# Gate and up of a decoder's feed-forward: weights as the stationary operand, both parts of the activations as the moving one

## The chip, the core and the metric

The kernel runs on one core of a Trainium2 chip. Its engines are TensorE (PE; matrix products, with its weight loads listed apart as PEld), VectorE (DVE), ScalarE (ACT), GpSimd (POOL) and SyncE (SP, which here issues the transfers from memory). Each works through its own list of instructions in order, and they wait for one another by semaphores. The metric is the time of one execution in microseconds (us) on the device; lower is better. All inputs are float32.

## The reference, cut to what matters

Two layers, each a mixer (attention) and a feed-forward, over a residual stream x of 256 tokens by 1024 columns. The mixers are left out here. The feed-forward's inner width D_FF is 2816.

```python
def rmsnorm(x, g):
    xf = x.astype(jnp.float32)
    y = xf * lax.rsqrt(jnp.mean(xf * xf, axis=-1, keepdims=True) + NORM_EPS)
    return (y * g.astype(jnp.float32)).astype(x.dtype)

def swiglu(h, w_gate, w_up, w_down):
    return (jax.nn.silu(h @ w_gate) * (h @ w_up)) @ w_down

def reference(...):
    for layer in range(DEPTH):          # DEPTH = 2
        h = rmsnorm(x, norm_mix[layer])
        ...                             # the mixer of this layer
        x = x + mix
        x = x + swiglu(rmsnorm(x, norm_ffn[layer]), ffn_w_gate[layer], ffn_w_up[layer], ffn_w_down[layer])
    return rmsnorm(x, norm_final)
```

## The kernel before

**Three products for one.** To keep float32's precision, each operand is split in a high part (a copy to the type fp32r, made by ACT) and a low part (the value less the high part, made by DVE). A product is then three products on PE: high by high, high activation by low weight, low activation by high weight (`mm3`, L264).

**A product on PE** has a stationary operand of 128 x 128, which a weight load brings in, and a moving operand of up to 512 columns that streams through it. The result stands in PSUM, eight banks of 128 partitions x 512 float32. The kernel shares them out: four banks `mm` (gate and the outputs), two banks `s` (up), two banks `tp` (transposes).

**Weights** come as one stream of tiles of 128 x 1024 (class `Weights`, L74): a transfer fills w_raw (5 buffers), ACT copies it to w_hi (L108), DVE subtracts into w_lo (L109; 7 buffers each). `W.next()` hands out the next tile and has up to six more prepared. The list of tiles follows FF_CHUNKS; a chunk of width w has 1024 / w slices of the model width in one tile.

**The norm** (`Norm.half`, L226) takes one half of 512 columns of one block of 128 tokens as soon as the residual of that half is done: DVE multiplies by the gain (xg, L229), PE transposes it in four blocks (pt_a, L215), ACT and DVE split it into aT, where the model width is on the partitions (L209, L210). The scale of each token, rs, comes later from the sum of squares (ACT, DVE, POOL); products use the unscaled activations and multiply rs in afterwards. aT has a tile for each block of tokens t and each part: four tiles.

**The feed-forward** (`ffn`, L322) goes chunk by chunk through the inner units: five chunks of 512 and one of 256. For gate and then for up, the stationary operand is a block of aT (128 tokens), the moving one 512 columns of weights, so the result has tokens on the partitions and inner units along the row. Then for each t ACT takes Silu of gate with the scale rs of the token (sg, L343), DVE multiplies up by rs and by sg (hn, L344), and since the down product needs inner units on the partitions, PE transposes hn in blocks of 128 (`split_T`, L215), and ACT and DVE split that into hT_hi and hT_lo. The transposes of a chunk run on PE among the first products of the next chunk.

**The down product** (`residual`, L281) has a block of hT stationary and 512 columns of the down weights moving; its last three tiles are done half by half, so that each half's residual (x, L302) and the next norm start early.

**Order.** The order in which each engine runs its list is set by a scheduler of the framework, which places instructions by its own estimate of times; transfers stay in program order.

## Time and profile before

| | |
|---|---|
| time, median of 3 runs | 676.5 us (675.41 to 676.85) |
| the profiled execution, its own time | 676.92 us |
| its span, first to last instruction | 675.1 us |
| granted PE clock, mean | 0.993 of full speed |
| first gate product to first down product, layer 0 | 143.52 to 270.35 us |
| the same, layer 1 | 480.86 to 607.42 us |

The profile is of one execution. Times are counted from the span's start. Busy time is the time an engine worked on something; on PE the ends of products are modelled and overlap, so the distance from start to start says more than the duration. A row of a timeline has the start, the duration, engine, line, operation, output <- inputs and the shape, and in brackets how long the engine had been idle and what ended that. In grouped rows stand busy us, mean ns of one, then the idle time ahead.

### The profile page before, as it was taken

The numbers are of one execution on the slowest core, as the hardware profiler recorded it, in microseconds if no ns is written. First come the engines' busy times: TensorE is split into PE (matmuls) and PEld (weight loads), VectorE is DVE, ScalarE is ACT, GpSimd is POOL, SyncE is SP. The second block draws the span as 40 slices with busy tenths as digits, with TensorE's granted clock in tenths as the row PEclk, the third lists the DMA queues.
The fourth block names the chain that finished last, engine by engine and source line by source line (L and its number), as shares of the span: only waits on it lengthen the run. The fifth ranks groups of instructions, "written<-read, shape, count | busy, mean of one in ns | idle before, by whom it ended". The sixth has DMA issues, their size and how long they took to land.

```text
span 675.1 us, 9324 instructions
## 1 busy us (share of the span) xinstructions
PE 651.3 (96%) x3329; PEld 533.7 (79%) x3329; DVE 435.6 (65%) x954; ACT 369.5 (55%) x671; POOL 12.4 (2%) x24
## 2 busy tenths in 40 slices
PE   5999999999999999999999999969999999999996
PEld 4979788778888889888887877746788888898884
DVE  4989977767455555543588899696674555465424
ACT  4775847547444444433376687686574544444322
POOL 1000000100000000000000000000000000000000
PEclk9999999999999999999999999989999999999999
DMA  8845355138666666662386431400396555555501
GB/s 313 254 149 168 117 165 157 31 109 319 201 184 184 192 182 184 185 193 74 101 346 216 155 126 39 150 0 2 121 329 196 178 178 196 181 182 187 186 1 62
DMA packets 31869, 109.62 MB, mean 162 GB/s; under 512 B 3536, under 2 KB 3792, under 8 KB 31568
## 3 DMA queue, kind: packets, MB, share of 16 engines
q1 hardware_dynamic: 31392, 108.45, 49.5%
q8 instruction: 26, 0.43, 0.3%
q10 hardware_dynamic: 432, 0.59, 0.2%
q14 instruction: 19, 0.16, 0.1%
HBM read 107.98 MB, written 1.05 MB: 161 GB/s over the span
## 4 chain that ended last, share of the span: by engine, by line
PE 82%; ACT 6%; DMA 5%; DVE 4%; issue 2%; POOL 0%; SPq 0%; POOLq 0%; DVEq 0%; ACTq 0%
PE ps_out L265 7%; PE ps_out L267 7%; PE ps_out L266 7%; PE ps_g L267 5%; PE ps_g L266 5%; PE ps_g L265 5%; PE ps_u L266 5%; PE ps_u L267 5%; PE ps_u L265 5%; DMA w_raw<-in_w 5%; PE ps_in L265 4%; PE ps_in L267 4%; PE ps_in L266 4%; PE pt_a L215 3%; PE ps_o L822 2%
## 5 line engine op out<-in xcount | busy, mean ns | idle before, releaser
L109 DVE TENSOR_TENSOR w_lo<-w_raw,w_hi 128x1024 fp32r<-128x1024 f32 (+5 forms) x200 | 234.5, 1180 | 176.6 <-ACT w_hi L108 176.2
L108 ACT ACTIVATE w_hi<-w_raw 128x1024 fp32r<-128x1024 f32 (+5 forms) x200 | 202.9, 1024 | 203.4 <-PE ps_out L267 58.6
L265 PE MATMUL ps_in<-w_hi,aT 128*128 128x512 f32 (+5 forms) x208 | 77.5, 373 | 1.2 <-ACT aT L209 1.2
L267 PE MATMUL ps_in<-w_hi,aT 128*128 128x512 f32 (+5 forms) x208 | 77.2, 373 | 0.0
L266 PE MATMUL ps_in<-w_lo,aT 128*128 128x512 f32 (+5 forms) x208 | 76.7, 370 | 0.0
L265 PE MATMUL ps_g<-w_hi,aT 128*128 128x512 f32 (+1 forms) x192 | 72.4, 377 | 0.0
L267 PE MATMUL ps_g<-w_hi,aT 128*128 128x512 f32 (+1 forms) x192 | 71.8, 376 | 0.0
L266 PE MATMUL ps_g<-w_lo,aT 128*128 128x512 f32 (+1 forms) x192 | 71.7, 373 | 0.0
L265 PE MATMUL ps_u<-w_hi,aT 128*128 128x512 f32 (+1 forms) x192 | 71.3, 371 | 0.0
L266 PE MATMUL ps_u<-w_lo,aT 128*128 128x512 f32 (+1 forms) x192 | 71.3, 371 | 0.0
L267 PE MATMUL ps_u<-w_hi,aT 128*128 128x512 f32 (+1 forms) x192 | 71.3, 371 | 0.0
L265 PE MATMUL ps_out<-w_hi,hT_hi 128*128 128x512 f32 x176 | 69.5, 395 | 0.0
L267 PE MATMUL ps_out<-w_hi,hT_lo 128*128 128x512 f32 x176 | 69.3, 394 | 0.0
L266 PE MATMUL ps_out<-w_lo,hT_hi 128*128 128x512 f32 x176 | 68.5, 389 | 0.0
L265 PEld LDWEIGHTS ps_in<-w_hi,aT 128*128 128x128 f32 x208 | 39.9, 192 | 6.1 <-ACT aT L209 1.8
L320 ACT ACTIVATE e<-e,bias 128x128 f32<-128x128 f32 (+1 forms) x96 | 42.5, 446 | 3.1 <-DVE bias L319 3.0
L267 PEld LDWEIGHTS ps_in<-w_hi,aT 128*128 128x128 f32 x208 | 39.7, 191 | 4.5 <-DVE aT L210 0.3
L266 PEld LDWEIGHTS ps_in<-w_lo,aT 128*128 128x128 f32 x208 | 39.7, 191 | 4.4 <-issue 0.4
L265 PEld LDWEIGHTS ps_u<-w_hi,aT 128*128 128x128 f32 x192 | 36.2, 188 | 6.3
L266 PEld LDWEIGHTS ps_u<-w_lo,aT 128*128 128x128 f32 x192 | 36.2, 188 | 6.3
L267 PEld LDWEIGHTS ps_u<-w_hi,aT 128*128 128x128 f32 x192 | 36.2, 188 | 6.2
L265 PEld LDWEIGHTS ps_g<-w_hi,aT 128*128 128x128 f32 x192 | 36.2, 188 | 6.0
(208 smaller groups left out, 946.2 us busy)
## 6 DMA issues: line engine op xcount, KB each, us to landing
w_raw<-in_w SPq DMA_DIRECT2D x176, 512.0 KB, 3.6
w_raw<-in_w SPq DMA_DIRECT2D x8, 384.0 KB, 4.6
gain<-in_vec SPq DMA_DIRECT2D x4, 512.0 KB, 5.1
cw<-in_cw SPq DMA_DIRECT2D x2, 1024.0 KB, 8.2
w_raw<-in_w SPq DMA_DIRECT2D x4, 416.0 KB, 6.6
w_raw<-in_w SPq DMA_DIRECT2D x4, 328.0 KB, 6.9
w_raw<-in_w SPq DMA_DIRECT2D x4, 304.0 KB, 2.8
x<-in_x SPq DMA_DIRECT2D x4, 256.0 KB, 6.2
```

The costliest lines, as they stand in the source:

```text
L108: nc.scalar.activation(hi[:, :n], raw[:, :n], AF.Copy)
L109: nc.vector.tensor_sub(lo[:, :n], raw[:, :n], hi[:, :n])
L215: TE.transpose(pt[:, i], src[:, i * P : (i + 1) * P], ident)
L265: TE.matmul(ps, act[0][:, k], wh, start=start, stop=False)
L266: TE.matmul(ps, act[0][:, k], wl, start=False, stop=False)
L267: TE.matmul(ps, act[1][:, k], wh, start=False, stop=stop)
L320: A.activation(e, e, AF.Exp, scale=-1.0, bias=bias, accum_out=den)
L822: pin(TE.matmul(ob[64 * par : 64 * par + 64], vv[:, st, c : c + 64], pTs[par][:, b, st].rearrange("p j c -> p (j c)"), start=False, stop=l ...
```

## The change

Gate and up change roles: a block of 128 x 128 weights is stationary and the activations move, so inner units come out on the partitions, as the down product wants them, and the transposes of hn go. The activations of both parts and all 256 tokens lie in one tile aW (`new_wide`): for the high weights one product moves 512 columns (256 tokens of the high part, 256 of the low part), for the low weights one moves the 256 of the high part. High by high and low weight by high activation meet in the left half of the bank, high weight by low activation in the right half, so the two halves must be added: an ACT copy of the right half and a DVE addition, for gate and for up. The token's scale now lies along the row; it is spread over the partitions once per layer (`spread`: two products of a block of ones with a diagonal of rs), multiplied into gate by DVE, and for up it is put off to the end of the down product (`residual` with rs). All chunks are 256 wide.

```diff
@@ -27,7 +27,7 @@
 
 EV_CHUNKS = [328, 416, 384, 384, 512, 512, 512]
 OD_CHUNKS = [304, 256, 512, 512, 512, 512]
-FF_CHUNKS = [512, 512, 512, 512, 512, 256]
+FF_CHUNKS = [256] * 11
 WCOLS = 1024
 
 
@@ -205,6 +205,11 @@
     def new_aT(pool):
         return [[pool.tile([P, KD, P], F32R, tag="aT", bufs=2 * NT, name="aT") for _ in range(2)] for _ in range(NT)]
 
+    def new_wide():
+
+        w = ap.tile([P, KD, 2, T], F32R, tag="aW", name="aW")
+        return w, [[w[:, :, z, t * P : (t + 1) * P] for z in range(2)] for t in range(NT)]
+
     def split(hi, lo, src):
         A.activation(hi, src, AF.Copy)
         V.tensor_sub(lo, src, hi)
@@ -220,7 +225,7 @@
 
         def __init__(self, goff):
             self.goff = goff
-            self.aT = new_aT(ap)
+            self.wide, self.aT = new_wide()
             self.rs = [small_tile(1, "rs") for _ in range(NT)]
 
         def half(self, t, h):
@@ -278,7 +283,7 @@
                     mm3(ps[t][:, :w], aT[t], g * kk + i, wh[:, i], wl[:, i], g == 0 and i == 0, g == n - 1 and i == kk - 1)
         return ps
 
-    def residual(act, nk, tail, nxt):
+    def residual(act, nk, tail, nxt, rs=None):
 
         ps = [[mm_bank("ps_out") for _ in range(2)] for _ in range(NT)]
 
@@ -299,7 +304,10 @@
                     one(t, h, nk - tail + k, last[k])
                 if t == NT - 1 and h == 1:
                     W.prepare(W.used + 2)
-                V.tensor_add(xs[t][:, c], ps[t][h], xs[t][:, c])
+                if rs is None:
+                    V.tensor_add(xs[t][:, c], ps[t][h], xs[t][:, c])
+                else:
+                    V.scalar_tensor_tensor(xs[t][:, c], ps[t][h], rs[t], xs[t][:, c], op0=ALU.mult, op1=ALU.add)
                 nxt.half(t, h)
 
     def rope(pool, dst, src, rs, t, nb, d):
@@ -320,31 +328,58 @@
         A.activation(e, e, AF.Exp, scale=-1.0, bias=bias, accum_out=den)
 
     def ffn(nm, goff):
-        aT, rs = nm.aT, nm.rs
+        wide, rs = nm.wide, nm.rs
         gain(goff)
         nxt = Final() if goff == V_FIN else Norm(goff)
         with tc.tile_pool(name="ffn", bufs=1, reuse_waits="tile") as fp:
-            hT = [(fp.tile([P, KF, P], F32R, tag=f"hh{t}", name="hT_hi"), fp.tile([P, KF, P], F32R, tag=f"hl{t}", name="hT_lo")) for t in range(NT)]
-            k0 = 0
-            for c, w in enumerate(FF_CHUNKS):
+            hh = fp.tile([P, KF, T], F32R, tag="hh", name="hT_hi")
+            hl = fp.tile([P, KF, T], F32R, tag="hl", name="hT_lo")
+
+
+            ones = fp.tile([P, P], F32, tag="ones", name="ones")
+            V.memset(ones, 1.0)
+            rB = fp.tile([P, T], F32, tag="rB", name="rB")
+
+            def spread():
+                dg = nat("dg")
+                pb = t_bank("ps_r")
+                for t in range(NT):
+                    c = slice(t * P, (t + 1) * P)
+                    V.tensor_scalar(dg[:, c], ident, rs[t], None, op0=ALU.mult)
+                    TE.matmul(pb[:, c], ones, dg[:, c], start=True, stop=True)
+                evac(rB, pb[:, :T])
+
+            f0 = 0
+            for w in FF_CHUNKS:
                 kk = ff_kk(w)
-                n = KD // kk
-                gp = [mm_bank("ps_g") for _ in range(NT)]
-                up = [s_bank("ps_u") for _ in range(NT)]
+                nf = w // P
+                gp = [mm_bank("ps_g") for _ in range(nf)]
+                up = [s_bank("ps_u") for _ in range(nf)]
                 for dst in (gp, up):
-                    for g in range(n):
+                    for g in range(KD // kk):
                         wh, wl = W.next()
                         for i in range(kk):
-                            for t in range(NT):
-                                mm3(dst[t][:, :w], aT[t], g * kk + i, wh[:, i], wl[:, i], g == 0 and i == 0, g == n - 1 and i == kk - 1)
-                for t in range(NT):
-                    sg = fp.tile([P, 512], F32, tag="sg", bufs=2, name="sg")[:, :w]
-                    hn = fp.tile([P, 512], F32, tag="hn", bufs=2, name="hn")[:, :w]
-                    A.activation(sg, gp[t][:, :w], AF.Silu, scale=rs[t])
-                    V.scalar_tensor_tensor(hn, up[t][:, :w], rs[t], sg, op0=ALU.mult, op1=ALU.mult)
-                    split_T(hT[t], k0, hn, w // P)
-                k0 += w // P
-            residual(hT, KF, 3, nxt)
+                            k = g * kk + i
+                            for f in range(nf):
+                                c = slice(f * P, (f + 1) * P)
+                                TE.matmul(dst[f], wh[:, i, c], wide[:, k].rearrange("p z q -> p (z q)"), start=k == 0, stop=False)
+                                TE.matmul(dst[f][:, :T], wl[:, i, c], wide[:, k, 0], start=False, stop=k == KD - 1)
+                    if dst is gp and f0 == 0:
+                        spread()
+                for f in range(nf):
+                    sg = fp.tile([P, T], F32, tag="sg", bufs=3, name="sg")
+                    hn = fp.tile([P, T], F32, tag="hn", bufs=3, name="hn")
+                    evac(sg, gp[f][:, T:])
+                    V.tensor_add(sg, gp[f][:, :T], sg)
+                    V.tensor_mul(sg, sg, rB)
+                    A.activation(sg, sg, AF.Silu)
+                    evac(hn, up[f][:, T:])
+                    V.tensor_add(hn, up[f][:, :T], hn)
+                    V.tensor_mul(hn, hn, sg)
+                    split(hh[:, f0 + f], hl[:, f0 + f], hn)
+                f0 += nf
+            hT = [[z[:, :, t * P : (t + 1) * P] for z in (hh, hl)] for t in range(NT)]
+            residual(hT, KF, 3, nxt, rs)
         return nxt
 
 
```

What this does to the order of PE at the entry of the first feed-forward, first before, then after: ps_out are the last products of the mixer's output, pt_a <- xg the transposes of the second 128 tokens, ps_g the first gate products. Waits stand in brackets with the engine waited for.

```order
L265 MATMUL ps_out<-w_hi,aT 128x512
L266 MATMUL ps_out<-w_lo,aT 128x512
L267 MATMUL ps_out<-w_hi,aT 128x512
L265 MATMUL ps_g<-w_hi,aT 128x512 [waits Activation_49]
L215 MATMUL pt_a<-con,xg 128x128 [waits DVE_49,PE_49]
L215 MATMUL pt_a<-con,xg 128x128 x3
L266 MATMUL ps_g<-w_lo,aT 128x512
L267 MATMUL ps_g<-w_hi,aT 128x512
L265 MATMUL ps_g<-w_hi,aT 128x512
L266 MATMUL ps_g<-w_lo,aT 128x512
L215 MATMUL pt_a<-con,xg 128x128 [waits DVE_49,PE_49]
```

```order
L270 MATMUL ps_out<-w_hi,aT 128x512
L271 MATMUL ps_out<-w_lo,aT 128x512
L272 MATMUL ps_out<-w_hi,aT 128x512
L220 MATMUL pt_a<-con,xg 128x128 [waits DVE_49,PE_49]
L220 MATMUL pt_a<-con,xg 128x128 x3
L220 MATMUL pt_a<-con,xg 128x128 [waits DVE_49,PE_49]
L220 MATMUL pt_a<-con,xg 128x128 x3
L365 MATMUL ps_g<-aW,w_hi 128x512 [waits DVE_49]
L366 MATMUL ps_g<-aW,w_lo 128x256
L365 MATMUL ps_g<-aW,w_hi 128x512
L366 MATMUL ps_g<-aW,w_lo 128x256
```

Before, gate products on the first 128 tokens stand among the transposes of the second 128; after, both groups of transposes and a wait for DVE stand ahead of the first gate product.

DVE's list in the first feed-forward, in the middle of it, is next; first before, where one chunk of 512 has two pieces hn and two pieces hT_lo:

```order
L344 SCALAR_TENSOR_TENSOR hn<-ps_u,rs,sg 128x512 [waits PE_49] x2
L109 TENSOR_TENSOR w_lo<-w_raw,w_hi 128x1024 [waits DMAHW6_49,Activation_49]
L210 TENSOR_TENSOR hT_lo<-pt_a,hT_hi 128x512 [waits Activation_49] x2
L109 TENSOR_TENSOR w_lo<-w_raw,w_hi 128x1024 [waits DMAHW7_49,Activation_49]
L109 TENSOR_TENSOR w_lo<-w_raw,w_hi 128x1024 [waits DMAHW0_49,Activation_49]
L109 TENSOR_TENSOR w_lo<-w_raw,w_hi 128x1024 [waits DMAHW1_49,Activation_49]
L109 TENSOR_TENSOR w_lo<-w_raw,w_hi 128x1024 [waits DMAHW2_49,DVE_49,Activation_49]
L109 TENSOR_TENSOR w_lo<-w_raw,w_hi 128x1024 [waits DMAHW3_49,DVE_49,Activation_49]
L109 TENSOR_TENSOR w_lo<-w_raw,w_hi 128x1024 [waits DMAHW4_49,DVE_49,Activation_49]
L109 TENSOR_TENSOR w_lo<-w_raw,w_hi 128x1024 [waits DMAHW5_49,Activation_49]
```

And after, most of one chunk of 256 (it goes on with one more weight split and one more hT_lo): sg is gate, hn is up, ps_g and ps_u their banks, rB the spread scale.

```order
L373 TENSOR_TENSOR sg<-ps_g,sg 128x256 [waits Activation_49]
L374 TENSOR_TENSOR sg<-sg,rB 128x256 [waits DVE_49]
L109 TENSOR_TENSOR w_lo<-w_raw,w_hi 128x1024 [waits DMAHW0_49,PE_49,Activation_49]
L373 TENSOR_TENSOR sg<-ps_g,sg 128x256 [waits Activation_49]
L374 TENSOR_TENSOR sg<-sg,rB 128x256 [waits DVE_49]
L109 TENSOR_TENSOR w_lo<-w_raw,w_hi 128x1024 [waits DMAHW1_49,PE_49,Activation_49]
L377 TENSOR_TENSOR hn<-ps_u,hn 128x256 [waits Activation_49]
L378 TENSOR_TENSOR hn<-hn,sg 128x256 [waits DVE_49]
L109 TENSOR_TENSOR w_lo<-w_raw,w_hi 128x1024 [waits DMAHW2_49,PE_49,Activation_49]
L215 TENSOR_TENSOR hT_lo<-hn,hT_hi 128x256 [waits Activation_49]
L377 TENSOR_TENSOR hn<-ps_u,hn 128x256
L378 TENSOR_TENSOR hn<-hn,sg 128x256 [waits DVE_49]
```

Between one weight split (w_lo) and the next there now stand one to three pieces of 256 columns, most with a wait for ACT (Activation), where weight splits followed one another.

## Rows read from the trace of the kernel before

**Rows 1.** Page part 1: busy us (share of the span) xinstructions.

```profile
PE 651.3 (96%) x3329; PEld 533.7 (79%) x3329; DVE 435.6 (65%) x954; ACT 369.5 (55%) x671; POOL 12.4 (2%) x24
```

**Rows 2.** Windows: length, busy of PE, PEld, DVE, ACT, POOL, clock, DMA, GB/s.

```profile
143.52:270.35 126.83, 126.65 (x626) 106.00 (x624) 71.72 (x73) 64.65 (x75) 1.12 (x2) 1.00 0.66 207
480.86:607.42 126.56, 126.56 (x626) 106.01 (x624) 71.75 (x73) 64.60 (x75) 1.09 (x2) 1.00 0.62 208
507.51:530.31 22.80, 22.80 (x106) 18.75 (x105) 12.32 (x12) 10.90 (x12) 0.00 (x0) 1.00 0.56 184
```

**Rows 3.** Timeline of PE, first gate chunk of layer 1.

```profile
484.71 0.39 PE L265 MATMUL ps_g<-w_hi,aT 128*128 128x512 f32 x1
...
499.67 0.39 PE L265 MATMUL ps_u<-w_hi,aT 128*128 128x512 f32 x1
```

**Rows 4.** Timeline of PE, the chunk of 256 of layer 1.

```profile
597.10 0.28 PE L266 MATMUL ps_g<-w_lo,aT 128*128 128x256 f32 x1
...
607.18 0.28 PE L266 MATMUL ps_u<-w_lo,aT 128*128 128x256 f32 x1
```

**Rows 5.** Timeline of PE around the transposes of one chunk.

```profile
526.77 0.39 PE L266 MATMUL ps_g<-w_lo,aT 128*128 128x512 f32 x1
527.06 0.66 PE L215 MATMUL pt_a<-con,hn 128*128 128x128 f32 x4
...
528.46 0.39 PE L266 MATMUL ps_g<-w_lo,aT 128*128 128x512 f32 x1
```

**Rows 6.** Timeline of PE in the second mixer, fp32 products of 128 columns.

```profile
469.44 1.06 PE L814 MATMUL ps_o<-cT,vbd 128*128 128x128 f32 x8
470.43 1.08 PE L822 MATMUL ps_o<-pT,vv 128*64 128x512 f32 x4
```

**Rows 7.** Timeline at the entry of the second feed-forward.

```profile
480.86 0.40 PE L265 MATMUL ps_g<-w_hi,aT 128*128 128x512 f32 x1
...
481.78 0.69 DVE L229 TENSOR_TENSOR xg<-x,gain 128x512 f32<-128x512 f32 x1
...
482.44 0.69 DVE L210 TENSOR_TENSOR aT<-pt_a,aT 128x512 fp32r<-128x512 f32 x1
...
482.62 0.63 PE L215 MATMUL pt_a<-con,xg 128*128 128x128 f32 x4
...
484.02 0.40 PE L265 MATMUL ps_g<-w_hi,aT 128*128 128x512 f32 x1
...
484.88 0.55 POOL L199 TENSOR_TENSOR rs<-rs,half 128x1 f32<-128x1 f32 x1 [3.48 <-DVE rs L198]
```

**Rows 8.** Grouped rows of DVE and ACT, by form.

```profile
L109 DVE TENSOR_TENSOR w_lo<-w_raw,w_hi 128x1024 fp32r<-128x1024 f32 x176 | 213.9, 1222 | 166.0 <-ACT w_hi L108 165.5
...
L210 DVE TENSOR_TENSOR hT_lo<-pt_a,hT_hi 128x256 fp32r<-128x256 f32 x4 | 1.5, 415 | 0.0
...
L108 ACT ACTIVATE w_hi<-w_raw 128x1024 fp32r<-128x1024 f32 x176 | 185.1, 1058 | 186.0 <-PE ps_out L267 50.8 <-PE ps_u L267 50.5 <-PE ps_g L267 41.4
...
L343 ACT ACTIVATE sg<-ps_g,rs 128x256 f32<-128x256 f32 x4 | 1.9, 470 | 3.0 <-PE ps_g L267 3.0
...
L209 ACT ACTIVATE hT_hi<-pt_a 128x256 fp32r<-128x256 f32 x4 | 1.3, 371 | 0.0
```

**Rows 9.** Waits, 484 to 596 us: total us, times, longest us.

```profile
ACT w_hi L108 <- PE ps_u L267: 22.9, 14, 1.7
...
ACT w_hi L108 <- DMA w_raw<-in_w: 3.6, 2, 2.7
```

**Rows 10.** Grouped rows of DVE: residual and the old hn.

```profile
L344 DVE SCALAR_TENSOR_TENSOR hn<-ps_u,rs,sg 128x512 f32<-128x512 f32 x20 | 14.0, 744 | 0.0
...
L302 DVE TENSOR_TENSOR x<-ps_out,x 128x512 f32<-128x512 f32 x16 | 11.0, 689 | 14.2 <-PE ps_out L267 14.1
```

**Rows 11.** Grouped row of PE's weight loads.

```profile
L265 PEld LDWEIGHTS ps_u<-w_hi,aT 128*128 128x128 f32 x192 | 36.2, 188 | 6.3
```

## The prediction

> **What bounds the kernel now.** I read the engine totals of the page first. TensorE (PE) is busy 651.3 us (96% of the span) and VectorE (DVE) 435.6 (65%) [rows 1]. That busy PE is a share only; whether PE is the limit in the part that changes is read from stretches. The two stretches from the first gate product to the first down product last 126.83 and 126.56 us, and PE is busy in 126.65 and 126.56 of them, at granted clock 1.00 (the 2.4 GHz level) [rows 2]. So gate and up wait for nothing: their time is what PE is given to do. One chunk of 512 inner units takes 22.80 us there, of which DVE works 12.32 (54%) and ScalarE (ACT) 10.90 (48%) [rows 2]. The reader should keep two things: a PE instruction saved in this stage is time saved, and DVE and ACT have slack that the change is going to use.
>
> The sum is made against the profiled execution, 676.92 us (span 675.1, 1.8 outside it); the median of the three runs is 676.5, 0.4 less.
>
> **Matmuls: the same columns, cut differently.** I read the spacing of starts, since the recorded durations overlap. From 484.71 to 499.67 us lie 66 products of 512 columns: 14.96 / 66 = 0.2267 us each [rows 3]. From 597.10 to 607.18 lie 84 of 256 columns: 10.08 / 84 = 0.1200 us each [rows 4]. Columns at 2.4 GHz would be 0.2133 and 0.1067, so each product carries about 0.0133 us of its own, whatever its width.
> Before, a layer has five chunks of 96 products at 512 and one chunk of 96 at 256: 480 x 0.2267 + 96 x 0.1200 = 120.3 us. After, each of 22 unit blocks of 128 takes, for gate and for up and for each of 8 slices of the model width, one product of 512 columns (high weights; high and low activations side by side) and one of 256 (low weights; high activations): 352 pairs x (0.2267 + 0.1200) = 122.0 us. That is **+1.7 us a layer**: columns are equal (270,336), and 704 products carry their fixed part where 576 did. Bounds: without a fixed part for the added products 0.0; with the load of every pair laid bare far more (last rival). I take the two spacings added, since both stand in this stage.
>
> The Trainium skill, page "TensorE: Matmul & The Clock Gate", section "Back-to-back issue gap", gives N/2.4 + 2.5 ns between products. For 512 and 256 columns that is an estimate of 215.8 and 109.2 ns, where this trace has 226.7 and 120.0 [rows 3, 4]. By that page of the Trainium skill the step would be +0.3 us a layer instead of +1.7, and the whole sum 2.8 us better. The trace disagrees with it at both widths and decides, so +1.7 stays.
>
> **Transposes: gone.** Before, each chunk's hidden values come out with tokens on the partitions and PE turns them, 8 blocks per chunk of 512. Around one such pair of groups, three products that need 0.68 us take from 526.77 to 528.46, 1.69 us [rows 5]: 1.0 us for eight transposes; the chunk period says the same, 22.80 - 96 x 0.2267 = 1.04 [rows 2, 3]. Per layer five chunks at 1.03 and half of that for the last one, which falls into the down products: **-5.6 us a layer**. This is PE time in a stage where PE never waits, so it is path, all of it.
>
> **The broadcast of the row scale.** The change needs the scale of each token along the free axis and makes it with two fp32 products (ones times a diagonal) of 128 columns a layer. In the trace four such fp32 products (eight records) stand from 469.44 to 470.43, 0.25 us each [rows 6]: **+0.5 us a layer**. Its operand is ready long before: the second scale is done at 484.88 + 0.55 = 485.4 us [rows 7], and the first gate phase, 16 x 0.347 = 5.5 us, ends later (below). A bound above is one DVE-to-PE wait of about 1 us.
>
> **The entry into the feed-forward.** This is where something gets worse by order. Before, the first gate product needs only the first 128 tokens, and PE fills the wait for the second 128 with it: from 480.86 to 484.02 us PE issues nine products (2.04 us) and two groups of transposes, so 1.12 us go beside products [rows 7]. After, a moving operand holds both parts and all 256 tokens, so all transposes stand ahead of the first gate product. From the rows: the second group of transposes follows xg of 481.78 to 482.47 and starts at 482.62; DVE then takes the low part of the third of the four halves (of the second 128 tokens the first 512 columns) at 482.44 to 483.13 [rows 7]. A small memset (ones) now stands in DVE before that xg, say 0.15 to 0.2 us. So the first gate product starts near 483.45, 2.59 us after 480.86 and not 1.12 with products between: **+1.5 us a layer**. The next need, the fourth half of the activations, comes 2.8 us later (16 products) and is split about 484.8, ahead of need 486.2. Bounds: 1.3 (no memset) to 2.5 (one more DVE item of 0.69 ahead of the split).
>
> **The longer epilogue.** Per chunk of 256 units DVE gets four weight splits (1.222 each) and ten pieces of 128 x 256 at 0.415: 4.9 + 4.2 = 9.0 us, and ACT four weight copies (1.058), six copies of 256 columns (0.371) and two Silu (0.470): 4.2 + 2.2 + 0.9 = 7.4 us [rows 8]. A chunk lasts 32 x 0.3467 = 11.1 us on PE, so both fit, DVE at 82% where it had 54%. What PE waits for is the two banks of up, which the next chunk's up wants 5.55 us after this one ends. Following DVE's new order from that end: ACT copy of the first block 0.5, add and multiply 0.8, a weight split 1.2 (its copy on ACT runs beside), low part 0.4, second add 0.4, with handoffs 3.7 us. Margin 1.8 us, so steady chunks cost nothing. The weights keep their lead: a weight copy waits for PE to give buffers back (22.9 us in 14 waits), hardly for DMA (3.6 us, 2 waits) [rows 9]. Those two waits are at the stage's start, where ACT's copies of the gate banks now stand behind a weight copy; there the margin shrinks to about nothing in the first two chunks, and I allow 0.2 us a layer (bounds 0 and 1.5). Adding the scale in the down stage's last step costs DVE 0.744 instead of 0.689 [rows 10]; only the very last one is on the path, +0.06 in total.
>
> **Sum.** Per layer -5.6 + 1.7 + 0.5 + 1.5 + 0.2 = -1.7 us, twice -3.4, plus 0.06: -3.4. From 676.92 that is 673.5; less the 0.4 by which the median is below that execution, **673.1 us**. Mixers and down products keep their order but for a few rows at the entry of the second mixer, and SP issues the same transfers in the same order, so I put nothing there.
>
> **Rivals.**
> *DVE becomes the pace (slower).* Place: DVE's queue in a steady chunk, 14 items of which the four weight splits each wait for ACT and six pieces wait for ACT as well. It decides once waits inside that queue pass 11.1 - 9.0 = 2.1 us per chunk that cannot be used otherwise. Every 0.1 us beyond costs 22 x 0.1 = 2.2 us; at 2.5 us of waits it is 0.4 x 22 = +8.8, some 682 us. For it: each wait on ACT is a handoff, and the order is fixed. Against: ACT's weight copies, which the splits follow, wait before for PE [rows 9]: slack, not work; and the walk through a chunk above ends DVE in time.
> *The start eats the gain (no change).* In the first two chunks of each layer ACT waits for weight DMA (longest 2.7 us in the second layer [rows 9]) and now holds the copies of the gate banks, DVE's adds and up's banks behind it; a bank late by 1.5 us in each layer is 3.0 us: 676.1. For it: my margin there is near zero. Against: the transfers start at the same events as before, and what arrives late is wanted only some 11 us after the stage's first product.
> *The fixed part does not add (faster than forecast).* If the alternation hides the fixed part of the added products, the step is 0.0 (its lower bound) and the time 2 x 1.7 us better: 669.7. Against: both widths show the part when they stand alone [rows 3, 4].
> *Weight loads come out (much slower).* A load record lasts 0.188 us [rows 11], longer than the short product. Were it not hidden behind the product of 256 columns, each pair would take 0.188 - 0.120 = 0.068 more, 704 x 0.068 = +48: 721 us. Against: products of 256 columns, each with its own load, follow one another every 0.120 [rows 4], so loads overlap one another and the products. The Trainium skill, page "TensorE: Matmul & The Clock Gate", section "The mechanism" (packing), says that a load overlaps running products only where it goes to another row group. By that rule of the Trainium skill a load would show at every product here, before and after, and added products would pay it again; the trace has 0.0133 us beside the columns, so the rule as it stands does not hold for this stream.
>
> **How the numbers follow.** Forecast 0.72, its own range 671.5 to 675.2 (entry 1.3 to 2.5, epilogue 0 to 0.8). DVE's pace 0.10, start 0.13, no fixed part 0.03, loads 0.02. Measurement of this kernel tells about 0.2% (1.35 us) from no change. Faster by more than that, below 675.15: nearly all of the forecast (0.71), the 0.03 and a little of the start's case: 0.75. Same: most of the start's case and the forecast's end, 0.13. Slower: DVE's pace, the loads, none else: 0.12. The range must let go of no more than 2 in 10: 670.8 to 676.9 leaves out the slow rivals, the far end of the start's case and some of the better end.
>
> **What would show it.** Right: no transposes of hn; in the gate and up stretch starts alternating 0.227 and 0.120; stretches near 125.3 us from the end of the last mixer product to the first down product, against 126.6 to 126.8; one gap of some 1.3 us on PE before the first gate product. Wrong: PE waiting for the DVE add of hn (up's banks) in chunk after chunk; pairs spaced over 0.35; a granted clock under 1.00 in the stage after the gap at the entry; waits of ACT for w_raw that spread past the second chunk.

## The result, and what the profile shows after the change

The changed kernel takes **672.83 us** (median of 4 runs, 672.43 to 673.69), the kernel before beside it 676.23 (4 runs, 675.41 to 676.85): ratio 0.9946, 95% interval 0.9927 to 0.9965. The forecast was 673.1, in a range of 670.8 to 676.9. The number came out; the reasons did so only in part. In the two profiled executions nearly all of the difference lies outside the feed-forward, and when the same two kernels were timed again the ratio was 0.9968 (0.9941 to 0.9996) and then 1.0001 (0.9980 to 1.0022).

The page of the changed kernel, part 1 (answers to [rows 1]):

```profile
PE 646.6 (96%) x3505; PEld 537.5 (80%) x3505; DVE 492.2 (73%) x1132; ACT 394.8 (59%) x801; POOL 12.4 (2%) x24
```

DVE rises from 65% to 73%, and PE has 176 more products and 4.7 us less busy time. The stage itself, by windows (columns as in [rows 2]): slot after the last mixer product to the first down product of layer 0, then first gate product to first down product of both layers.

```profile
141.62:268.86 127.24, 126.27 (x718) 109.31 (x717) 98.84 (x159) 76.70 (x139) 1.11 (x2) 1.00 0.66 207
143.94:268.86 124.92, 124.92 (x710) 108.47 (x709) 96.59 (x154) 75.49 (x136) 0.56 (x1) 1.00 0.68 211
479.03:603.95 124.92, 124.92 (x709) 108.39 (x709) 96.87 (x154) 75.39 (x136) 0.55 (x1) 1.00 0.65 211
```

Before, the first gate product stood in that slot, so 127.24 stands against 126.83 and 126.56 [rows 2]: the stage has become longer, by 0.4 and 0.7 us, where 1.3 less was forecast. PE is busy in all of the 124.92, so nothing waits; the products themselves take longer than the sum had them. TensorE's timeline in the first up phase of layer 1 (start, us, engine, line, operation; answers to [rows 3, 4]):

```profile
488.05 0.40 PE L365 MATMUL ps_u<-aW,w_hi 128*128 128x512 f32 x1
488.29 0.28 PE L366 MATMUL ps_u<-aW,w_lo 128*128 128x256 f32 x1
488.41 0.40 PE L365 MATMUL ps_u<-aW,w_hi 128*128 128x512 f32 x1
...
488.76 0.40 PE L365 MATMUL ps_u<-aW,w_hi 128*128 128x512 f32 x1
...
489.11 0.40 PE L365 MATMUL ps_u<-aW,w_hi 128*128 128x512 f32 x1
...
489.47 0.40 PE L365 MATMUL ps_u<-aW,w_hi 128*128 128x512 f32 x1
```

A pair is one product of 512 and one of 256 columns; a phase is gate or up of one chunk, 16 pairs. Four pairs from 488.05 to 489.47 are 0.355 each; over whole phases (5.653 us) it is 0.3533, where 0.3467 was forecast. The pairs are not equal: 0.36, 0.35 and 0.35 us follow one another in turn (361, 349 and 350 ns in the trace, 1.060 us for three).

The entry into the second feed-forward (answers to [rows 7]):

```profile
476.48 0.40 PE L272 MATMUL ps_out<-w_hi,aT 128*128 128x512 f32 x1
476.99 0.63 PE L220 MATMUL pt_a<-con,xg 128*128 128x128 f32 x4
477.58 0.17 DVE L340 MEMSET ones<- 128x128 f32 x1
477.66 0.67 DVE L234 TENSOR_TENSOR xg<-x,gain 128x512 f32<-128x512 f32 x1
478.29 0.69 DVE L215 TENSOR_TENSOR aW<-pt_a,aW 128x512 fp32r<-128x512 f32 x1
478.48 0.63 PE L220 MATMUL pt_a<-con,xg 128*128 128x128 f32 x4 [0.86 <-DVE xg L234]
479.03 0.50 PE L365 MATMUL ps_g<-aW,w_hi 128*128 128x512 f32 x1
```

From the slot at 476.71 to the first gate product at 479.03 are 2.32 us (2.59 forecast), and the order of events is the one forecast: memset, xg, then the transposes beside the low part. The broadcast of the scale takes 484.79 to 485.15:

```profile
484.79 0.60 PE L349 MATMUL ps_r<-dg,ones 128*128 128x128 f32 x4
485.15 0.47 PE L365 MATMUL ps_u<-aW,w_hi 128*128 128x512 f32 x1
```

Waits of 484 to 596 us (answers to [rows 9]): the two waits of ACT for weight DMA are still 3.5 us and have not spread, and no wait of PE for up's banks is listed.

```profile
ACT w_hi L108 <- PE ps_u L365: 10.7, 9, 1.5
...
DVE hn L377 <- ACT hn L190: 6.2, 9, 0.7
ACT w_hi L108 <- DMA w_raw<-in_w: 3.5, 2, 2.6
```

So where do the 3.8 us between the two spans (675.13 and 671.35) lie? Read from the starts of TensorE's products: the first mixer's last product starts at 143.29 before and 141.39 after (-1.90); from there to the first product of the second mixer 189.67 and 189.30 (-0.37); from that to the last mixer product 147.67 and 145.79 (-1.88); to the last down product 187.46 and 187.68 (+0.22); the end +0.14. **The feed-forwards give -0.15, the mixers, which the change hardly touches, -3.8.** For the second mixer the granted clock says why. Windows of the kernel before:

```profile
443.00:453.00 10.00, 4.79 (x22) 3.00 (x23) 9.68 (x48) 8.43 (x29) 0.00 (x0) 0.87 0.00 0
453.00:463.00 10.00, 10.00 (x47) 6.67 (x46) 7.14 (x34) 6.35 (x20) 0.00 (x0) 0.79 0.01 2
```

The same place of the changed kernel:

```profile
441.00:451.00 10.00, 4.60 (x24) 2.90 (x25) 9.68 (x50) 8.54 (x30) 0.00 (x0) 1.00 0.01 2
451.00:461.00 10.00, 10.00 (x59) 7.31 (x57) 9.24 (x46) 8.48 (x27) 0.00 (x0) 1.00 0.00 0
```

In both, PE has a hole there: it works 4.8 and 4.6 of 10 us, waiting mostly for DVE's pieces of the softmax (sc 2.4 us, e 1.7 and 1.8 us). Before, part of these 20 us was granted at the 1.2 GHz level, and PE got 47 products done in the second window; after, it stayed at 2.4 GHz and got 59 done. For the first mixer the weights are the likely cause. The last wait for them in the chain of waits (start, us, what) ends at 36.59 before and 31.78 after, and the rest of that mixer runs behind it: 106.70 us before, 109.61 after, so the two are not the same step of it. In ten of the fourteen profiles, of both kernels, the mixer's last product starts 109.6 to 109.7 us behind that landing. The kernel before:

```profile
29.80 6.79 DMA w_raw<-in_w
```

The changed kernel:

```profile
25.33 6.45 DMA w_raw<-in_w
```

Whether either belongs to the change is what the first experiments ask.

### The profile page after: what moved, and what is told of

Its sections match the earlier page's. It is cut to its first block, busy times and chain, and to the rows that moved or that the text cites. A ratio compares the mean times of both kernels' runs of the same rounds, so it can differ in the third digit from the quotient of the medians.

```text
span 671.4 us, 10018 instructions
## 1 busy us (share of the span) xinstructions
PE 646.6 (96%) x3505; PEld 537.5 (80%) x3505; DVE 492.2 (73%) x1132; ACT 394.8 (59%) x801; POOL 12.4 (2%) x24
## 4 chain that ended last, share of the span: by engine, by line
PE 83%; DVE 6%; ACT 5%; DMA 3%; issue 2%; POOL 1%; SPq 0%; POOLq 0%; DVEq 0%; ACTq 0%
PE ps_g L365 12%; PE ps_u L365 12%; PE ps_out L272 7%; PE ps_out L271 7%; PE ps_out L270 7%; PE ps_u L366 6%; PE ps_g L366 6%; PE ps_in L270 4%; PE ps_in L271 4%; PE ps_in L272 4%; DMA w_raw<-in_w 3%; PE ps_o L857 2%; PE pt_p L841 2%; DVE w_lo L109 1%; ACT w_hi L108 1%
## 5 line engine op out<-in xcount | busy, mean ns | idle before, releaser
L365 PE MATMUL ps_g<-aW,w_hi 128*128 128x512 f32 x352 | 125.6, 399 | 0.0
L365 PE MATMUL ps_u<-aW,w_hi 128*128 128x512 f32 x352 | 125.5, 399 | 0.0
L366 PE MATMUL ps_u<-aW,w_lo 128*128 128x256 f32 x352 | 98.9, 281 | 0.0
L366 PE MATMUL ps_g<-aW,w_lo 128*128 128x256 f32 x352 | 98.9, 281 | 0.0
L365 PEld LDWEIGHTS ps_u<-aW,w_hi 128*128 128x128 f32 x352 | 66.2, 188 | 16.4
L270 PE MATMUL ps_in<-w_hi,aW 128*128 128x512 f32 (+5 forms) x208 | 77.5, 373 | 1.0 <-ACT aW L214 0.9
L272 PE MATMUL ps_in<-w_hi,aW 128*128 128x512 f32 (+5 forms) x208 | 77.0, 372 | 0.0
L271 PE MATMUL ps_in<-w_lo,aW 128*128 128x512 f32 (+5 forms) x208 | 76.6, 369 | 0.0
L366 PEld LDWEIGHTS ps_u<-aW,w_lo 128*128 128x128 f32 x352 | 66.5, 189 | 0.0
L366 PEld LDWEIGHTS ps_g<-aW,w_lo 128*128 128x128 f32 x352 | 66.5, 189 | 0.0
L270 PEld LDWEIGHTS ps_in<-w_hi,aW 128*128 128x128 f32 x208 | 39.8, 192 | 6.2 <-ACT aW L214 1.6
L272 PEld LDWEIGHTS ps_in<-w_hi,aW 128*128 128x128 f32 x208 | 39.6, 191 | 4.6 <-DVE aW L215 0.5
```

The costliest lines, as they stand in the source:

```text
L270: TE.matmul(ps, act[0][:, k], wh, start=start, stop=False)
L271: TE.matmul(ps, act[0][:, k], wl, start=False, stop=False)
L272: TE.matmul(ps, act[1][:, k], wh, start=False, stop=stop)
L365: TE.matmul(dst[f], wh[:, i, c], wide[:, k].rearrange("p z q -> p (z q)"), start=k == 0, stop=False)
L366: TE.matmul(dst[f][:, :T], wl[:, i, c], wide[:, k, 0], start=False, stop=k == KD - 1)
```

## The experiments

Ratios are to the kernel before, timed beside each run, with the 95% interval. Stretches of all profiles, read from the starts of TensorE's products (us): start of the last product of the first mixer; first gate to first down product of each layer; first to last product of the second mixer.

| kernel | first mixer | gate and up | second mixer |
|---|---|---|---|
| before | 143.29 | 126.83, 126.56 | 147.67 |
| before, again | 141.79 | 126.56, 126.57 | 148.64 |
| before, no turning | 142.06 | 121.44, 121.44 | 147.24 |
| before, holes filled | 143.36 | 126.56, 126.57 | 146.28 |
| changed | 141.39 | 124.92, 124.92 | 145.79 |
| changed, again | 142.24 | 124.92, 124.93 | 148.78 |
| changed, third | 142.25 | 124.92, 124.92 | 148.39 |
| changed, holes filled | 142.48 | 122.69, 122.69 | 146.37 |
| changed, holes filled, again | 142.63 | 124.92, 124.92 | 146.80 |
| changed, more DVE work | 143.22 | 124.92, 122.68 | 149.05 |
| changed, one width | 141.66 | 160.19, 160.18 | 147.38 |
| grouped | 142.40 | 123.45, 123.46 | 148.83 |
| grouped, entry in halves | 141.80 | 125.40, 125.40 | 147.92 |
| last version | 144.43 | 124.56, 124.56 | 147.42 |

In the kernels before and in the last two rows gate starts in the slot behind the mixer's last product; in the others 2.32 to 2.34 us later.

**The two kernels once more** (no edit).

> The kernel before, unchanged, for a second profile. In the first pair of profiles the feed-forward stretches (slot after the last mixer product to the first down product) went from 126.83 and 126.56 to 127.24 and 127.24, and what was gained stands in the mixers: even 143.52 to 141.62, odd (first projection product to the last output product) 147.90 to 146.02. Theory 'the change moves the mixers': this profile repeats 143.5 and 147.9 within 0.3, with the clock at 0.8 near 450 to 460 us. Rival 'one execution differs from another': it lands elsewhere, between 141.6 and 144 and between 146 and 148, and the clock falls at another place or not at all; the time stays within 675.4 to 676.9 only if the differences offset each other.

> The changed kernel, unchanged, for a second profile and for a time beside the others. 672.4 to 673.7 us by both theories. Theory 'the change moves the mixers': even mixer 141.6, odd mixer 146.0 again. Rival 'one execution differs from another': either of them moves by a us or more, with the clock or with the arrival of the first weights. Both: feed-forward stretches of 127.2 again, pairs of products every 0.353.

Measured: before 676.05 (8 runs, 673.63 to 677.93; ratio to the kernel before 0.9992, 0.9974 to 1.0011), changed 675.23 (10 runs, 669.10 to 677.71; ratio 0.9968, 0.9941 to 0.9996). The changed kernel's time lies above the 672.4 to 673.7 that both theories expected. Its gate and up stretches repeat to 0.01 us, and those of the kernel before to 0.01 us in three of four (the fourth, 126.83, has 0.2 us in which PE stands still). The mixers don't: the second takes 148.64 before and 148.78 after, with the clock down in both. The window of the changed kernel that read 1.00 above reads 0.77 here:

```profile
441.00:451.00 10.00, 5.36 (x21) 3.72 (x19) 8.65 (x45) 8.50 (x28) 0.00 (x0) 0.77 0.00 0
```

So "the change moves the mixers" falls; "one execution differs from another" stands. What the mixers gave in the first pair of profiles was not the change's. The Trainium skill, page "TensorE: Matmul & The Clock Gate", section "Part 1: The HAM clock gate (the "warmup" mystery)", says that what the clock gate goes by runs freely and is not reset when a kernel starts, so that one kernel meets it differently from run to run. The two windows of this one kernel, 1.00 and 0.77, are in line with that.

**Before, without turning (transposing) the hidden values.** The down products then read operands that lie wrong; the rest of the work is kept.

```diff
-                    split_T(hT[t], k0, hn, w // P)
+                    split(hT[t][0][:, k0 : k0 + w // P], hT[t][1][:, k0 : k0 + w // P], hn.rearrange("p (k c) -> p k c", c=P))
```

> The kernel before without the 44 transposes of the hidden values: hn is split as it lies, tokens on the partitions, so the down products get wrong operands; all other work is kept. Theory: the transposes are on the path whole, 5.6 us a layer, so 676.2 - 11.2 = 665.0 (664.4 to 665.6). Rival 'something else is late next' (weights or their copies): less than half of it shows, over 670.

Measured: 664.25 (4 runs), ratio 0.9821 (0.9797 to 0.9845), 12.1 us less. The first stretch, by windows (the second is 121.44 too):

```profile
142.29:263.73 121.44, 121.44 (x585) 102.23 (x584) 71.83 (x73) 64.07 (x75) 1.12 (x2) 1.00 0.67 217
```

126.56 to 121.44 is 5.12, and the down products of the second layer go from 60.67 to 60.19: 5.60 us in that layer, and 5.59 in the first against the kernel's second profile, the forecast's term. The rest of the 12.1 is within its interval.

**The order of the two widths.** Products are emitted per weight tile, all eight of 512 columns first.

```diff
-                        for i in range(kk):
+                        for z, i in [(z, i) for z in range(2) for i in range(kk)]:
...
-                                TE.matmul(dst[f], wh[:, i, c], wide[:, k].rearrange("p z q -> p (z q)"), start=k == 0, stop=False)
-                                TE.matmul(dst[f][:, :T], wl[:, i, c], wide[:, k, 0], start=False, stop=k == KD - 1)
+                                if z == 0: TE.matmul(dst[f], wh[:, i, c], wide[:, k].rearrange("p z q -> p (z q)"), start=k == 0, stop=False)
+                                if z == 1: TE.matmul(dst[f][:, :T], wl[:, i, c], wide[:, k, 0], start=False, stop=k == KD - 1)
```

> The changed kernel with the products of gate and up in another order: per weight tile all eight of 512 columns (high weights), then all eight of 256 (low weights), where they alternated. Theory 'the change of width costs': a pair took 0.353 where 0.2267 + 0.1200 = 0.3467 was forecast, and the 0.0063 is paid at the changes between widths; with one change in eight products a pair takes about 0.347 to 0.348, 704 x 0.0055 = 3.9 us less: 668.9 (668.4 to 669.5). Rival 'a 512-column product on the joined activations takes 0.235 in any order': no change, 672.8. Second rival 'short products in a row lay their loads bare': over 0.12 each, slower than 673.

Measured: 674.19 (10 runs, 673.32 to 675.16), ratio 0.9964 (0.9953 to 0.9976). TensorE's timeline, where eight like products make one row:

```profile
501.70 2.00 PE L365 MATMUL ps_u<-aW,w_hi 128*128 128x512 f32 x8
503.54 1.12 PE L366 MATMUL ps_u<-aW,w_lo 128*128 128x256 f32 x8
504.50 2.00 PE L365 MATMUL ps_g<-aW,w_hi 128*128 128x512 f32 x8
```

Eight pairs take 2.80, 0.350 each (0.349 over whole phases of 5.587): the stage is 1.47 us shorter, twice 1.47 = 2.9 of the 3.9 expected. The time misses the 668.9 expected by 5 us, since that was counted from the first median, 672.83, and this profile has a second mixer of 148.83. Against a pair of 0.3533 the alternation costs something, but not all that lies between 0.3533 and 0.3467 comes back. The short products do not lay their loads bare: 0.96 / 8 = 0.120.

**One width for both.**

```diff
-                                TE.matmul(dst[f][:, :T], wl[:, i, c], wide[:, k, 0], start=False, stop=k == KD - 1)
+                                TE.matmul(dst[f], wl[:, i, c], wide[:, k].rearrange("p z q -> p (z q)"), start=False, stop=k == KD - 1)
```

> The changed kernel with the low weights multiplied with both halves of the activations, 512 columns like the high weights (adds low times low, which the reference does not need; more columns, one width). Theory 'the change of width costs': with one width a product takes 0.2267 again, 704 x 0.2267 = 159.6, the gate and up stretch 160.2 us. Rival 'the joined operand costs 0.235 for 512 columns in any order': 704 x 0.236 = 166.1, stretch 166.8.

Measured: 745.51 (one run), stretches 160.19 and 160.18, the 160.2 of the first theory:

```profile
200.15 0.39 PE L365 MATMUL ps_u<-aW,w_hi 128*128 128x512 f32 x1
...
201.51 0.39 PE L365 MATMUL ps_u<-aW,w_hi 128*128 128x512 f32 x1
```

Six products in 1.36 us are 0.227, as in [rows 3]. The joined operand costs nothing by itself; the rival falls.

**The holes of the second mixer filled**, in both kernels, with idle products:

```diff
+    def fill(bank, gate, q, n):
+        if n:
+            TE.matmul(bank[:, : gate.shape[-1]], ident, gate, start=True, stop=True)
+        for _ in range(n):
+            pin(TE.matmul(bank, q[0][:, 0], q[0][:, :4].rearrange("p h c -> p (h c)"), start=True, stop=True))
+        return bank
...
-                    pt = t_bank("pt_c")
+                    pt = fill(t_bank("pt_c"), mx, qS, 7 * (gp == 1 and t == 1))
...
-                            pt = t_bank("pt_p").rearrange("p (g b k c) -> p g b k c", g=g, b=2, c=P)
+                            pt = fill(t_bank("pt_p"), den, qS, 4 * (gp == 1 and t == 0 and par == 1)).rearrange("p (g b k c) -> p g b k c", g=g, b=2, c=P)
```

> The kernel before with 15 idle products of 512 columns (and three tiny ones that hold them back until a row of DVE is done) put into the holes of TensorE in the second half of the odd mixer, in banks that are written anew right after; nothing is left out. For both theories the granted clock stays at the 2.4 GHz level there and the odd mixer lasts about 146 us (145.5 to 147) where it took 147.7 and 148.6; so 674 to 675.5. Theory 'the difference in time between the two kernels is the clock in this hole': the same edit on the changed kernel gives the same time, within 0.8 us. Rival 'the feed-forward itself is faster': the changed kernel stays 3.4 us below this one.

> The changed kernel with the same 15 idle products in the same places. Theory 'clock': feed-forward stretches before and after add up to the same (+2.32 entry, -1.64 gate and up, -0.80 and -0.45 down), so this lands within 0.8 us of the kernel before with the same edit, 674 to 675.5, and its times spread over less than the 8.6 us (669.1 to 677.7) that the changed kernel showed. Rival 'faster feed-forward': 3.4 us below it.

Measured: before 674.92 (10 runs, 673.66 to 675.78), ratio 0.9980 (0.9964 to 0.9997); changed 673.28 (10 runs, 669.70 to 675.79), ratio 0.9951 (0.9925 to 0.9976). Second mixer of the kernel before with the edit, first to last product:

```profile
332.76:479.04 146.28, 142.65 (x828) 110.25 (x827) 120.42 (x426) 104.35 (x264) 0.84 (x4) 1.00 0.34 124
```

The clock stays at 1.00 in both, and the mixers agree (146.28, 146.37): the hole is what let the clock fall. But neither time came as expected: the two kernels differ by 1.6 us, where 0.8 at most or 3.4 was expected, and the changed kernel's times still spread over 6.1 us, against 2.1 in the kernel before with the edit. In this profile the changed kernel has stretches that no other had shown:

```profile
145.04:267.73 122.69, 122.69 (x709) 108.15 (x709) 96.75 (x154) 75.42 (x136) 0.56 (x1) 1.00 0.70 214
478.46:601.15 122.69, 122.69 (x709) 108.16 (x709) 96.79 (x154) 75.46 (x136) 0.55 (x1) 1.00 0.64 215
```

The same code of gate and up, 2.23 us quicker in each layer, the products as many (x709) and the clock the same. Its timeline:

```profile
488.14 0.39 PE L372 MATMUL ps_u<-aW,w_hi 128*128 128x512 f32 x1
488.37 0.28 PE L373 MATMUL ps_u<-aW,w_lo 128*128 128x256 f32 x1
...
489.52 0.39 PE L372 MATMUL ps_u<-aW,w_hi 128*128 128x512 f32 x1
```

Four pairs in 1.38 us: 0.345; over whole phases of 5.547 it is 0.3467, the forecast's number.

**Is the cadence the build's?** The changed kernel and the filled one, unchanged, again; the cadence is the time that the pairs of a stage keep.

> The changed kernel, unchanged, for a third profile. In its first two profiles every pair of products in gate and up took 0.3537 us (phases of 5.65); in the profile of the same kernel with the filled holes every pair took 0.3473 (phases of 5.545), as the prediction had it, in both layers. Theory 'the pair has two cadences, and an execution keeps one of them': this profile shows phases of 5.65 or of 5.55, nothing between, the same in both layers, and the times of the runs spread by the 4.4 us between them (704 x 0.0064) beside what the clock takes. Rival 'the cadence belongs to the build': 5.65 again, as both times before.

> The changed kernel with the holes filled, once more, for a second profile. Theory 'an execution keeps one of two cadences': phases of 5.65 or of 5.55, the time near 674 with the one and near 670 with the other. Rival 'the cadence belongs to the build': 5.55 again and near 670.

Measured: changed 676.86 (8 runs, 674.71 to 678.80; ratio 1.0001, 0.9980 to 1.0022), filled 674.12 (8 runs, 672.70 to 675.42; ratio 0.9968, 0.9945 to 0.9990). The filled kernel, whose two stages took 122.69, now has:

```profile
145.20:270.12 124.92, 124.92 (x709) 108.46 (x709) 96.60 (x154) 75.42 (x136) 0.56 (x1) 1.00 0.69 211
```

Its two profiled executions took 670.32 and 675.42; of the 5.1 between them 4.5 are the two stages. One program, both cadences: the build does not decide.

**More work for DVE.**

```diff
-                    V.tensor_mul(hn, hn, sg)
+                    V.tensor_mul(hn, hn, sg); [V.tensor_mul(scr, hn, sg) for _ in range(2)]
```

> The changed kernel with two more multiplies of 128x256 into a scratch tile on VectorE for each block of 128 units (nothing is left out): per chunk of 256 units DVE gets 4 x 1.22 + 14 x 0.424 = 10.8 us instead of 9.1, where TensorE takes 11.1 or 11.3. Theory 'DVE has slack in the longer epilogue': the pieces disappear in it, and from the first gate to the first down product it stays 124.9 (or 122.7 at the quicker cadence) within 0.5. Rival 'DVE's queue is the pace as soon as its waits pass the slack': the waits on ACT, some 1.8 us per chunk in the profile of the changed kernel, come on top of 10.8, a chunk takes 12 to 12.6, the stretch 132 to 139, and TensorE waits for the add of hn in chunk after chunk.

Measured: 675.95 (one run). First gate to first down product:

```profile
145.77:270.69 124.92, 124.92 (x710) 108.53 (x709) 106.48 (x194) 75.85 (x136) 0.56 (x1) 1.00 0.67 210
484.11:606.79 122.68, 122.68 (x709) 108.25 (x709) 106.67 (x194) 76.34 (x136) 0.55 (x1) 1.00 0.66 214
```

DVE works 106.5 where it had 96.6, and PE still waits for nothing: the pieces vanish in the slack, and the rival falls. And here one execution has both cadences, one in each layer. So it is not a property of the execution either, as I had put it: a stage takes one behind its first phase and keeps it. In all twelve stages of the alternating order the first phase, with the broadcast at its end, takes 6.11 to 6.13; the next one 5.72 to 5.74 in nine of them and 5.64 in three; and then every phase 5.64 to 5.67, or 5.54 to 5.55. It is settled around the broadcast. Single pairs say more. The first gate phase runs in the pattern of three pairs (361, 349, 350 ns) in all twelve stages; at the quick cadence every pair takes 347 ns. What differs is where the pattern stands when the broadcast (ps_r) breaks in. The filled kernel's first profile, quick behind it:

```profile
483.51 0.40 PE L372 MATMUL ps_g<-aW,w_hi 128*128 128x512 f32 x1
...
483.87 0.40 PE L372 MATMUL ps_g<-aW,w_hi 128*128 128x512 f32 x1
...
484.22 0.60 PE L356 MATMUL ps_r<-dg,ones 128*128 128x128 f32 x4
```

The changed kernel's second profile, slow behind it:

```profile
487.90 0.40 PE L365 MATMUL ps_g<-aW,w_hi 128*128 128x512 f32 x1
...
488.25 0.40 PE L365 MATMUL ps_g<-aW,w_hi 128*128 128x512 f32 x1
...
488.61 0.61 PE L349 MATMUL ps_r<-dg,ones 128*128 128x128 f32 x4
```

In all three quick stages the long pair (0.36) is the last but one ahead of the broadcast; in the nine slow ones it is the last (seven) or the third from last (two). That parts the twelve without exception, but it was read afterwards and no run set it on purpose; why it should matter is open.

**The entry.** Grouped, and of gate's first weight tile all products in token halves:

```diff
+                        parts = [slice(t * P, (t + 1) * P) for t in range(NT)] if dst is gp and f0 == 0 and g == 0 else [slice(0, T)]
+                        for q in parts:
...
+                                    o = dst[f].rearrange("p (z q) -> p z q", z=2)
+                                    if z == 0: mmi = TE.matmul(o[:, :, q], wh[:, i, c], wide[:, k, :, q], start=k == 0 and q.start == 0, stop=False, skip_group_check=True)
+                                    if z == 1: mmi = TE.matmul(o[:, 0, q], wl[:, i, c], wide[:, k, 0, q], start=False, stop=k == KD - 1, skip_group_check=True)
...
```

> The grouped order, and the first weight tile of gate in each layer multiplied in two token halves: eight products of 2x128 columns and eight of 128 for the first 128 tokens, then the same for the second. Theory: TensorE waits some 1.5 of the 2.32 us between the last mixer slot and the first gate product, and the first half (8 x 0.12 + 8 x 0.07 = 1.5 us) fills that; the split costs 8 x 4 added products' fixed parts, 0.2 us. From the slot after the last mixer product to the first down product 124.7 us, where grouped has 126.0; twice 1.3 = 2.6 us below grouped. Rival 'the wait only moves': the second half then waits for the last split and the stretch stays at 125.7 or more.

Measured: 673.81 (10 runs, 672.00 to 676.41), ratio 0.9971 (0.9953 to 0.9989); 125.40 from the slot, where grouped has 125.78 and 124.7 was expected. PE does not wait, but the halves are dear:

```profile
479.57 0.98 PE L369 MATMUL ps_g<-aW,w_lo 128*128 128x128 f32 x7
480.38 1.16 PE L368 MATMUL ps_g<-aW,w_hi 128*128 128x256 f32 x8
481.37 1.01 PE L369 MATMUL ps_g<-aW,w_lo 128*128 128x128 f32 x8
482.22 2.07 PE L368 MATMUL ps_g<-aW,w_hi 128*128 128x512 f32 x8
```

Eight products of 128 columns take 0.85, 0.106 each, eight of 256 columns 0.99, 0.124. I had 0.07 for the narrow ones, 0.6 us too little for 16 of them, and of 1.3 us only 0.4 came back.

**The last version** takes what held: grouped order, filled holes, the memset once at the start, and at the entry only the high-weight products in halves.

```diff
+                    if dst is gp and f0 == 0:
+                        wt = [W.next(hold=g + 1) for g in range(2)]
+                        for g, z, q in ((0, 0, a0), (1, 0, a0), (0, 0, a1), (0, 1, aa), (1, 0, a1), (1, 1, aa)):
+                            mm(dst, wt[g], g, z, q)
```

(g is the weight tile, z = 0 the high weights, a0 and a1 the two token halves, aa both; mm is the loop of the grouped version for one of these.)

> The grouped order, the holes of the odd mixer filled as in the two runs with idle products, the memset of ones once at the start, and another entry: of the first chunk's gate the high-weight products go in token halves (16 of 2x128 columns for the first 128 tokens, then the second 128), the low-weight products stay 256 wide, since those of 128 columns took 0.106 to 0.124, no less than those of 256. Theory: from the slot after the last mixer product to the first down product 126.0 (grouped) less 1.3 = 124.7; odd mixer 146.3; sum 671 (669.8 to 672). Rival 'the cadence of the two halves or of the grouped order also has two values': spread of more than 3 us, median 672 or more.

Measured: **670.34** (4 runs, 668.62 to 672.40), ratio 0.9903 (0.9869 to 0.9938), 6.6 us below the kernel before by that ratio. The spread, 3.8 us, is over the 3 us of the rival, but the median is not over its 672:

```profile
144.66:269.22 124.56, 124.56 (x734) 110.33 (x732) 93.81 (x158) 77.10 (x139) 1.12 (x2) 1.00 0.70 212
```

From the slot to the first down product 124.56 (124.7 expected), against 126.56 before: 2.0 us a layer that are the feed-forward's own; the other 2.6 of the 6.6 lie outside. Its second mixer is 0.6 to 1.1 us longer than in the other filled profiles at a clock of 1.00, and its first is the longest of all; why is open.

## Why the prediction came out, step by step

| step, us a layer | forecast | measured, nine stages of twelve | three of twelve |
|---|---|---|---|
| matmuls | +1.7 | 352 x 0.3533 - 120.3 = +4.1 | 352 x 0.3467 - 120.3 = +1.7 |
| transposes | -5.6 | -5.6 | -5.6 |
| broadcast | +0.5 | 6.12 - 5.65 = +0.5 | +0.5 |
| entry | +1.5 | 2.32 - 1.12 = +1.2 | +1.2 |
| epilogue | +0.2 | 0.0 | 0.0 |
| sum | -1.7 | +0.2 | -2.2 |

- **Matmuls: the step that failed.** "I take the two spacings added, since both stand in this stage" takes two steady streams of one width each for a stream that alternates. It holds in three stages of twelve; in nine a pair takes 0.0066 us more, 2.3 us a layer. The text itself named it ("pairs spaced over 0.35" as wrong), but the bounds stopped at 0.0 below and the loads above, and no rival had it. Direct reading of the whole feed-forward, from the mixer's last product to the next stage, agrees: -0.1 and +0.2 us in the two layers of the changed kernel's first profile, against the second profile of the kernel before; -2.3 and -2.0 in the filled kernel's first profile, against the kernel before with the same edit.
- The Trainium skill, page "TensorE: Matmul & The Clock Gate", section "Back-to-back issue gap", gives N/2.4 + 2.5 ns as the gap of single products; taken for this stream, a pair would be an estimate of 0.325 us and the products of the stage some 114.4. The trace disagrees, as before the change: the quickest pairs take 0.3467, 122.0 us of products.
- **Transposes:** right, shown by taking them away, to 0.1 us.
- **Entry, epilogue, broadcast:** right in their mechanism; the entry was put 0.3 too high, the epilogue 0.2, the broadcast as it came. The margin forecast for up's banks held even with 10 us more DVE work a stage.
- **Mixers: "I put nothing there".** Right for the change, wrong for the comparison: their length differs by 3 us from one execution to another, through the clock in the hole of the second and, by what the chain of waits shows, the arrival of the first weights in the first.
- **The sum** of -3.4 met the measured -3.4, but in the profiled execution that was luck: there the feed-forwards give -0.15 and the mixers -3.8. Of the other three of the first four runs only span and mean clock are known. Their clocks, 0.989 to 0.992, are those of the second and third profiles (0.990 and 0.992), in which the hole had let the clock fall, yet their spans are 670.6 to 671.8 where those two have 675.2 and 674.8; of the kernel before, no listed run at such a clock is under 673.5. Two quick stages give 2 x 2.23 = 4.5 us, so these runs were probably fast by the forecast's own sum; without a profile that is not shown. Of the three comparisons one shows 0.5% less, one 0.3%, one nothing; a mixture of +0.2 and -2.2 us a layer is what the stages explain.
- **Rivals:** DVE's pace and the bare loads are shown not to hold; the start took nothing (waits for DMA 3.5 us, 3.6 before); "the fixed part does not add" did not hold in any stage, and in nine the error lay the other way.

## What to carry to other kernels

Compare two kernels stage by stage, in more than one execution of each: a stage that repeats to 0.01 us carries the verdict, and one that differs by microseconds between executions of the same kernel carries none, however well the total fits. Cost a mixed stream from a mixed stream: here the sum of the two pure ones, 0.3467, was the lower of two values, and the higher held in nine stages of twelve. Products of one width kept together gave the steadier time here (0.349 in all six stages), not the lowest. A wait at the entry of a stage can be filled with the part of its products whose operands are there, if the pieces are not cut so narrow that a product's time hardly shrinks any more (here 128 columns).

## What the runs showed of the hardware that was not expected

- Products of 512 and 256 columns in turn run at 0.3533 or 0.3467 us a pair at the same clock of 1.00, each kept from the second phase to the end of the stage (336 pairs); the slower is a pattern of 361, 349 and 350 ns, the quicker is even; in runs of eight they take 0.349 in all six stages seen, and 512 alone 0.227.
- A product of 128 columns took 0.106, hardly less than one of 256 (0.120). The Trainium skill, page "TensorE: Matmul & The Clock Gate", section "LDWEIGHTS (loading the stationary operand)", gives a load P/1.2 ns for P columns, an estimate of 107 ns here. The 0.106 agrees with it; that the load is what paces these products no run here shows.
- Fifteen idle products in a hole of some 10 us kept the granted clock at the 2.4 GHz level, in both kernels and all four filled profiles. Without them it was down to the 1.2 GHz level for some of that hole in every profile but the changed kernel's first.
